# Decoder layer: first projection by column halves of the modulation, key compression earlier in the filler, MLP operands of the second token half in two steps

## Chip, cores, metric

One core of a Trainium2 chip (trn2) runs the whole kernel as one program. The metric is device time in microseconds: the median over runs of the program.

## What is computed

One layer of a decoder trunk, 1024 tokens of width 1024, in float32. Cut to what matters:

```python
mod = silu(c) @ ada_w + ada_b                        # 1024 -> 6 x 1024
sh_a, sc_a, gt_a, sh_m, sc_m, gt_m = split(mod, 6)
h = rmsnorm(x, norm_mix_g) * (1 + sc_a) + sh_a
(a_q, a_k, a_v, b_q, b_k, b_v, b_f, c_q, c_k, c_v,   # 2960 columns in all
 d_q, d_kc, d_vc, d_ks, d_vs, d_kw, d_vw, d_g) = split(h @ w_in)
o_a = diff_attention(rmsnorm(a_q), rmsnorm(a_k), a_v)   # four groups of 4 heads x 64
o_b = forgetting_attention(...)
o_c = stick_breaking_attention(c_q, c_k, c_v)
o_d = native_sparse_attention(...)  # keys compressed: 32 positions, stride 16, @ phi_w
x = x + gt_a * (concat(o_a, o_b, o_c, o_d) @ w_out)
h = rmsnorm(x, norm_ffn_g) * (1 + sc_m) + sh_m
gate, val = split(h @ w_up)                          # 2 x 2816
x = x + gt_m * ((silu(conv3(gate) + conv_b) * val) @ w_down)
```

## The kernel before

**How the order is made.** `Program` records every engine operation in the order in which the code calls it; that number is its priority, to which `K.bias` is added. A list scheduler then fixes an order of instructions for each engine, from planned durations, before the kernel is built; on the chip each engine goes through its list in order. All compute instructions are issued from one recording line, L393 (L400 in the changed file). A tile belongs to a class with a quota (table in lines 547 to 563), and the tiles of one class are handed out in the order in which the program asks for them: in `try_alloc` a tile gets its buffer only if `c["ptr"] == t.order`. Dependencies are found per tile by the byte ranges that operations read and write (`region`). The eight PSUM banks form one group; in the first phase `Xa` and `X` have them, then `S` (4 banks), `T` (2), `O` (1) and `pP` (1), in the end phases `op`, `ox`, `oy`, `up` and `dn`.

**Precision.** An operand of a projection or of the MLP is kept as two tiles, a rounded one (hi) and the remainder (lo), and each product is three matmuls: hi·hi, lo·hi, hi·lo. With eight 128-row pieces of width 1024 (k 0 to 7) a block of 128 tokens takes 24 matmuls per projection.

**Front (lines 637 to 742, 1320 to 1330).** `load_x` brings four blocks of x and normalizes them. `ada_part(1)` loads the 1024 scale columns of `ada_w` in eight tiles `ada` of 128x1024 and sums them, each times a column of silu(c), into `acc` on VectorE; `ada_cols` turns the sum into columns by matmuls with a vector of ones into bank `Xa`. Then `ada_part(0)` does the same for the shift, in the single `acc`. `norm_x` transposes x by `ident` into bank `X`, and `modulate` (736) makes hx on ScalarE and hT hi and lo, the latter on VectorE or GpSimd. The first projections are A's queries (`p_aq`, 256 columns, weights `wh`), A's values (`p_va`, 256, weights `vw`), then 400 columns of C's and D's values with B's forget logits and D's gate logits (`vcd`), then A's keys: each block's sum in an `S` bank. `split_w` (759) makes weights hi on ScalarE and lo on GpSimd. `ada_rest` (1376) mixes the other four parts of the modulation into these projections, one step for 9.0 us of them.

**Attention and its filler.** After that `merge` (1287) mixes the attention of group A, then C, D and B, with `side()` (1393): the remaining projections one after another, `cq`, `ck`, `dk` (D's compressed keys and values and their window parts), `dq`, `cmp` (the compression itself), `vb`, `bq`, `bk`, then the output projection. The sums of these projections go to the one bank `pP`, and so does `pk`, the sum of the compression (line 1067); their raw tiles are of class `nt`. The compression forms X = keys + position embedding on VectorE and multiplies it by `phi` (128 paired matmuls).

**MLP (lines 1465 to 1606).** For each half of the tokens (512), four blocks of the output projection, residual and norm (`xn`), transposes into `oy`, modulation, and `split_b` into operands: `gA` from the first half, and from the second half sums and differences, `gB`, for a scheme of seven products in place of eight. `up_first` makes weights 1 and 2 of an f block (they multiply `gA`), `up_rest` the other five; f 0 and 1 come ahead of the loop (`EARLY`).

## Time and profile before

| | |
|---|---|
| median of 3 runs | 1467.6 us (1467.43 to 1468.78) |
| the profiled execution: its time | 1466.37 us |
| its span | 1464.5 us |
| mean granted TensorE clock | 0.973 |
| PE (matmul) busy | 1375.4 us, 94% of the span |
| PEld (weight load), DVE (VectorE) | 1169.1 us, 1100.9 us |
| ACT (ScalarE), POOL (GpSimd) | 717.6 us, 198.0 us |

PE is TensorE. A busy time is the union of an engine's instructions; idle time is put down to the instruction or transfer whose signal ended it. A share over the whole span is a mean over stages with different limits, so the stages are read one by one: the front to 200 us (modulation, first projections), A and C with the filler, D and B, the turn to the MLP near 811 us, and the MLP to the end. The granted clock is a fraction of TensorE's full 2.4 GHz; it is either full or half of that at a time, and a number between is a mix.

### The profile page before, as it was taken

Reading aid. Unit: us, or ns where it says so; the run is one execution under the profiler, and the core shown is the slowest. Engines: PE = TensorE matmul, PEld = TensorE weight load, DVE = VectorE, ACT = ScalarE, POOL = GpSimd, SP = SyncE. Lnnn points to the kernel's source line nnn. Section 1 sums busy time; section 2 is a strip of 40 time slices with the busy share of each in tenths; the row PEclk is TensorE's granted clock in tenths of the full one; section 3 lists DMA queues with packets and bytes.
Section 4 is the critical chain, followed back from the end, with each engine's and each line's share of the span. In section 5 each row is a group of like instructions: output and inputs, shape, how many; then the busy total and the mean of one; then the engine's idle time right before and its main releaser. Section 6 shows DMA issues by size and latency. Waiting matters only on the chain.

```text
span 1464.5 us, 24046 instructions
## 1 busy us (share of the span) xinstructions
PE 1375.4 (94%) x8573; PEld 1169.1 (80%) x8573; DVE 1100.9 (75%) x2301; ACT 717.6 (49%) x1547; POOL 198.0 (14%) x225
## 2 busy tenths in 40 slices
PE   3999999989799999999999699999999999999998
PEld 2879998888589887787788578888888888888887
DVE  7955669988788987577866976666666665898787
ACT  2530256657587765445754644444334344443242
POOL 4633120222223364100000000000000000000000
PEclk6799999999899999999999899999999999999999
DMA  9579463635421445433335132222222225963665
GB/s 358 198 228 304 153 167 107 179 88 145 122 67 52 123 154 160 143 100 92 82 105 190 64 104 87 77 76 78 86 87 87 83 90 202 373 208 100 230 248 171
DMA packets 169961, 211.22 MB, mean 144 GB/s; under 512 B 25517, under 2 KB 112214, under 8 KB 169842
## 3 DMA queue, kind: packets, MB, share of 16 engines
q1 hardware_dynamic: 168338, 208.52, 45.0%
q0 software_dynamic: 1504, 1.17, 0.4%
q8 instruction: 67, 1.10, 0.3%
q14 instruction: 52, 0.43, 0.1%
HBM read 165.30 MB, written 47.89 MB: 146 GB/s over the span
## 4 chain that ended last, share of the span: by engine, by line
PE 61%; DVE 9%; ACT 2%; issue 1%; DMA 1%; POOL 0%; SPq 0%; POOLq 0%; DVEq 0%; ACTq 0%
PE up L393 29%; PE dn L393 13%; PE T L393 5%; PE pP L393 5%; DVE P L393 4%; PE O L393 3%; PE op L393 3%; PE S L393 3%; ACT P L393 1%; DVE m L393 1%; DVE S L393 1%; DVE pt L393 0%; DVE gB L393 0%; DMA dg<-d_g 0%; PE oy L393 0%
## 5 line engine op out<-in xcount | busy, mean ns | idle before, releaser
L393 PE MATMUL up<-gB,fw 128*128 128x512 f32 x1320 | 306.0, 391 | 12.0 <-DVE fw L393 10.3
L393 PEld LDWEIGHTS up<-gB,fw 128*128 128x128 f32 x1320 | 248.7, 189 | 65.5 <-DVE fw L393 10.8
L393 PE MATMUL dn<-ds 128*128 128x512 f32 x924 | 210.3, 389 | 0.5 <-ACT ds L393 0.3
L393 PEld LDWEIGHTS dn<-ds 128*128 128x128 f32 x924 | 173.1, 188 | 37.4 <-DVE ds L393 1.0
L393 PE MATMUL pP<-wh,hT 128*128 128x256 f32 x1344 | 195.9, 289 | 1.3 <-ACT nt L393 0.7
L393 PEld LDWEIGHTS pP<-wh,hT 128*128 128x128 f32 x1344 | 176.0, 191 | 6.8 <-issue 1.9
L393 ACT ACTIVATE P<-S,nm 128x512 f32<-128x512 f32 (+3 forms) x240 | 135.3, 571 | 76.4 <-DVE nm L393 58.5
L393 PE MATMUL S<-kst,qst 128*128 128x512 f32 (+2 forms) x480 | 135.3, 370 | 6.4 <-DVE P L393 3.2
L393 PE MATMUL T<-ident,P 128*128 128x128 f32 x696 | 112.8, 281 | 17.5 <-ACT P L393 11.3
L393 PE MATMUL up<-gA,fw 128*128 128x512 f32 x528 | 124.5, 390 | 0.0
L393 PEld LDWEIGHTS up<-gA,fw 128*128 128x128 f32 x528 | 98.8, 188 | 20.3
L393 PEld LDWEIGHTS T<-ident,P 128*128 128x128 f32 x696 | 80.3, 141 | 37.0 <-ACT P L393 17.2
L393 PEld LDWEIGHTS S<-kst,qst 128*128 128x128 f32 x480 | 78.6, 193 | 17.3 <-DVE P L393 4.9
L393 ACT COPY pt<-T 128x512 f32<-128x512 f32 (+1 forms) x107 | 57.3, 542 | 61.1 <-PE T L393 59.0
L393 DVE TENSOR_REDUCE m<-S 128x1 f32<-128x512 f32 (+3 forms) x160 | 76.8, 490 | 8.9 <-PE S L393 8.5
L393 ACT CAST ds<-dg 128x512 fp32r<-128x512 f32 x82 | 48.1, 619 | 64.3 <-DVE dg L393 42.4
L393 DVE TENSOR_TENSOR fw<-fr,fw 128x512 fp32r<-128x512 f32 x110 | 75.0, 684 | 0.0
L393 DVE COPY pt<-T 128x512 f32<-128x512 f32 (+1 forms) x93 | 57.0, 623 | 21.4 <-PE T L393 19.9
L393 ACT CAST fw<-fr 128x512 fp32r<-128x512 f32 x110 | 67.5, 614 | 9.0 <-DVE fw L393 8.5
L393 ACT ACTIVATE P<-P 128x128 f32<-128x128 f32 (+8 forms) x98 | 64.8, 690 | 13.7 <-POOL P L393 11.2
L393 ACT COPY u<-up 128x512 f32<-128x512 f32 x44 | 25.9, 588 | 87.5 <-PE up L393 87.5
L393 DVE SCALAR_TENSOR_TENSOR cv<-ga,ccol,cv 128x1023 f32<-128x1023 f32 (+1 forms) x44 | 56.5, 1283 | 15.8 <-ACT cv L393 15.0
(286 smaller groups left out, 2341.1 us busy)
## 6 DMA issues: line engine op xcount, KB each, us to landing
dg<-d_g SPq DMA_DIRECT2D x99, 256.0 KB
fr<-in_ffn_w_up_dram SPq DMA_DIRECT2D x88, 256.0 KB
ada<-in_ada_w_dram SPq DMA_DIRECT2D x64, 256.0 KB
dg<-in_ffn_w_down_dram SPq DMA_DIRECT2D x55, 256.0 KB
d_g<-va SPq DMA_DIRECT2D x22, 512.0 KB
ada<-in_ada_w_dram SPq DMA_DIRECT2D x16, 512.0 KB
wr<-in_w_in_dram SPq DMA_DIRECT2D x32, 256.0 KB
x<-in_x_dram SPq DMA_DIRECT2D x8, 512.0 KB
```

Source lines behind the costliest of these rows:

```text
L393: return getattr(getattr(self.nc, eng), meth)(*a, **k)
```

## The change

1. **Front.** `ada_pair(h)` replaces `ada_part` here: one tile holds shift and scale columns of one half of the 1024 columns (128x2x512), so that eight loads of 512 KB and eight steps on VectorE give what k 0 to 3 of hT need (`pair_cols`), and eight more what k 4 to 7 need. `norm_x` comes in two parts accordingly. `acc` has two buffers.
2. **First projection.** A's queries and keys are one projection of 512 columns (`p_first`, weights in class `vw`), each block's sum in one bank; its weights are made in two steps (`cut`), lo on VectorE. Then come A's values with D's values and the logits (`vd`, 400 columns) and C's values (`CC_V`, 256). hT lo is always on VectorE. `ada_rest` gives one step for 6.0 us.
3. **Filler.** The order becomes `dk`, `cq`, `cmp`, `ck`, `dq`, `vb`, `bq`, `bk`; `pk` is in an `S` bank.
4. **MLP operands.** The second half of the tokens is done as two quarters of 256 columns, `split_b` writing a column range; `up_first(0)` and `up_first(1)` get a priority 300 places earlier. Dependencies know column ranges (`lane`).

The diff, cut to its core:

```diff
@@ class Program: dependencies also by columns
-        return self.p[0], self.p[1], lo, hi
+        return self.p[0], self.p[1], lo, hi, *self.lane
+
+    def columns(self, a, b):
+        v = self[(slice(None),) * len(self.shadow.shape) + (slice(a, b),)]
+        v.lane = a, b
+        return v
@@ classes
-            ("ada", 16, "b", 0), ("acc", 1, "b", 0), ("x", 8, "b", 0), ("hT", 16, "b", 1),
-            ("V", 4, "b", 1), ("VD", 1, "b", 1), ("vw", 8, "b", 1), ("vr", 2, "b", 1),
+            ("ada", 16, "b", 0), ("acc", 2, "b", 0), ("x", 8, "b", 0), ("hT", 16, "b", 1),
+            ("V", 4, "b", 1), ("VD", 1, "b", 1), ("vw", 8, "b", 1), ("vr", 4, "b", 1),
-            ("Xa", 2, "q", 0), ("X", 6, "q", 0), ("S", 4, "q", 1), ("T", 2, "q", 1), ("O", 1, "q", 1), ("pP", 1, "q", 1),
+            ("Xa", 1, "q", 0), ("X", 3, "q", 0), ("S", 4, "q", 1), ("T", 2, "q", 1), ("O", 1, "q", 1), ("pP", 1, "q", 1),
@@ front
+    def ada_pair(h):
+        acc = K.tile("acc", (128, 2, 512))
+        for k in range(8):
+            w = K.tile("ada", (128, 2, 512))
+            K.dma(w, dap(ada_w, k * 128 * 6 * D + h * 512, [[6 * D, 128], [D, 2], [1, 512]]), 524288)
+            if k == 0:
+                K.ts(acc, w, cact[:, k:k + 1], None, OP.mult)
+            else:
+                K.stt(acc, w, cact[:, k:k + 1], acc, OP.mult, OP.add)
+        return acc
+    def pair_cols(h, acc):
+        ps, k = ps1("Xa"), slice(4 * h, 4 * h + 4)
+        for u in (1, 0):
+            for c in range(4):
+                K.mm(ps[:, u * 4 + c:u * 4 + c + 1], acc[:, u, c * 128:(c + 1) * 128], ones[:, 0:1], True, True)
+        K.tt(a1_a[:, k], ps[:, 4:8], b_sc[:, k], OP.add)
+        K.tt(a1_a[:, k], a1_a[:, k], g_sc[:, k], OP.mult)
+        K.tt(sh_a[:, k], ps[:, 0:4], b_ada[:, k], OP.add)
-    def norm_x(half, xns):
-        for k in range(8):
+    def norm_x(half, xns, ks=range(8)):
+        for k in ks:
@@ modulate, split_w, proj
-        K.tt(lo(k, tk), hf, hi(k, tk), OP.subtract, ("DVE", "POOL"))
+        K.tt(lo(k, tk), hf, hi(k, tk), OP.subtract)
-        K.tt(lo, raw, hi, OP.subtract, ("POOL",))
+        K.tt(lo, raw, hi, OP.subtract, (eng,))
-            h, l = split_w(wcls, raw, (128, kp, n))
+            h, l = split_w(wcls, raw, (128, kp, n), "DVE" if cut else "POOL")
+            if cut and k0 + kp == 4:
+                yield 0
@@ first projections
-    p_aq = qk_proj("aq", CA_Q, g_aq, 32, True)
-    p_va = proj([(CA_V, 256)], 256, post_va, "vw", "vr", 4, True)
-    next(p_aq)
-    norm_x(0, x0)
-    next(p_va)
-    steps(p_aq, 4)
+    vd = [(CA_V, 256), (CD_VS, 64), (CD_VW, 64), (CB_F, 4), (CD_G, 12)]
+    p_first = proj([(CA_Q, 512)], 512, post_first, "vw", "vr", 2, True, True)
+    next(p_first)
+    norm_x(0, x0, range(0, 4))
+    acc1 = ada_pair(1)
+    next(p_first)
+    pair_cols(1, acc1)
+    norm_x(0, x0, range(4, 8))
+    steps(p_first, 4)
     norm_x(1, load_x(1))
-    steps(p_va, 4)
-                yield 9.0
+                yield 6.0
-    merge(ahead(p_aq, p_va, proj(vcd, 400, post_vcd, "vw", "vr", 2, True), qk_proj("ak", CA_K, g_ak, 32, True), begun=2),
+    merge(ahead(p_first, proj(vd, 400, post_vd, "vw", "vr", 2, True),
+                proj([(CC_V, 256)], 256, post_vc, early=True), begun=1),
           rest, 1.0)
@@ filler
-        pk = ps1("pP")
+        pk = ps1("S")
-        gs = [("cq", qk_proj("cq", CC_Q, 0.125)), ("ck", qk_proj("ck", CC_K, 1.0)), ("dk", compress()),
-              ("dq", qk_proj("dq", CD_Q, g_dq, 64)), ("cmp", compress_kv()), ("vb", proj([(CB_V, 256)], 256, post_vb)),
+        gs = [("dk", compress()), ("cq", qk_proj("cq", CC_Q, 0.125)), ("cmp", compress_kv()), ("ck", qk_proj("ck", CC_K, 1.0)),
+              ("dq", qk_proj("dq", CD_Q, g_dq, 64)), ("vb", proj([(CB_V, 256)], 256, post_vb)),
@@ MLP operands
-    for half in range(2):
-        xns = []
-        for q in range(4):
+    for half, g0, g1 in ((0, 0, 4), (1, 0, 2), (1, 2, 4)):
+        xns, cw = [], slice(g0 * 128, g1 * 128)
+        for q in range(g0, g1):
-            ps = ps1("oy")
+            ps = ps1("oy")[:, :cw.stop - cw.start]
-                opnd[5][r] = split_b("gB", t1)
+                split_b("gB", t1, 5, r, cw)
     for f in range(EARLY):
+        K.bias = -300.0
         up_first(f)
+        K.bias = 0.0
```

How this moves instructions, at three places.

The front, PE, from its first `Xa` matmuls on; `Xa<-ones,acc` turns a modulation sum into columns, `X<-ident,x` transposes x, `S<-wh,hT` and `S<-vw,hT` are projection products. Before:

```order
L393 MATMUL Xa<-ones,acc 128x1 x8
L393 MATMUL Xa<-ident,hx 128x7
L393 MATMUL Xa<-ones,acc 128x1 x8
L393 MATMUL X<-ident,x 128x128 x8
L393 MATMUL S<-wh,hT 128x256 x96
L393 MATMUL X<-ident,x 128x128 x6
L393 MATMUL S<-vw,hT 128x256 x5
L393 MATMUL X<-ident,x 128x128 x6
```

With the change:

```order
L400 MATMUL Xa<-ones,acc 128x1 x8
L400 MATMUL X<-ident,x 128x128 x16
L400 MATMUL S<-vw,hT 128x512 x39
L400 MATMUL Xa<-ones,acc 128x1 x8
L400 MATMUL S<-vw,hT 128x512 x3
L400 MATMUL Xa<-ident,hx 128x7
L400 MATMUL S<-vw,hT 128x512 x4
L400 MATMUL X<-ident,x 128x128 x4
L400 MATMUL S<-vw,hT 128x512 x50
```

Before, both `Xa` groups (scale, shift) stand ahead of the first product; now 39 products of 512 columns stand between the first and the second group.

The same place on DVE, from the first modulation sum on. With the change:

```order
L400 SCALAR_TENSOR_TENSOR acc<-ada,cact,acc 128x1024 x5
L400 TENSOR_TENSOR vw<-vr,vw 128x1024 x2
L400 TENSOR_TENSOR a_a<-Xa,b_sc 128x4
L400 TENSOR_TENSOR sh_a<-Xa,cols 128x4
L400 TENSOR_SCALAR acc<-ada,cact 128x1024
L400 TENSOR_TENSOR a_a<-a_a,g_sc 128x4
L400 SCALAR_TENSOR_TENSOR acc<-ada,cact,acc 128x1024
L400 CAST hT<-hx 128x512 x2
L400 TENSOR_TENSOR hT<-hx,hT 128x512 x2
```

Before, this place has sixteen sums of 128x1024 ahead of the first hT, and no `vw`; now eight sums of 128x1024, then two halves of the weights' lo, and hT follows two sums into the second pair.

PE around the key compression (`S<-nt,wr` or `pP<-nt,wr`; `V`, `P`, `pt`, `kst`, `qst` are tiles of the attention; `T<-ident,nt 128x32` is the transpose of the position embedding). Before, where it stands among the attention's work, behind all products of `dq`:

```order
L393 MATMUL O<-pt,V 64x128 x6
L393 MATMUL T<-ident,nt 128x128 x4
L393 MATMUL T<-ident,P 128x128 x2
L393 MATMUL S<-kst,qst 128x128 x2
L393 MATMUL T<-ident,P 128x128 x6
L393 MATMUL T<-ident,nt 128x32
L393 MATMUL S<-kst,qst 128x512 x2
L393 MATMUL O<-pt,V 64x128 x8
L393 MATMUL pP<-nt,wr 64x63
L393 MATMUL pP<-wr,nt 63x64
```

With the change, where products of the filler stand just ahead of it and it lies in A's attention:

```order
L400 MATMUL pP<-wh,hT 128x256 x24
L400 MATMUL T<-ident,P 128x128 x3
L400 MATMUL pP<-wh,hT 128x256 x9
L400 MATMUL O<-pt,V 64x128 x4
L400 MATMUL pP<-wh,hT 128x256
L400 MATMUL T<-ident,P 128x128 x6
L400 MATMUL T<-ident,nt 128x32
L400 MATMUL S<-kst,qst 128x512 x3
L400 MATMUL O<-pt,V 64x128 x6
L400 MATMUL S<-nt,wr 64x63
L400 MATMUL S<-wr,nt 63x64
```

The compression went from row 385 of PE's list to row 237, and from bank `pP` to an `S` bank.

PE at the start of the MLP (`op` the output projection, `ox` and `oy` transposes, `up<-gA` products that need the first half of the tokens, `up<-gB` those that need the second). Before:

```order
L393 MATMUL up<-gA,fw 128x512 x6
L393 MATMUL oy<-ident,xn 128x128 x3
L393 MATMUL up<-gA,fw 128x512 x19
L393 MATMUL oy<-ident,xn 128x128 x7
L393 MATMUL up<-gA,fw 128x512 x2
L393 MATMUL oy<-ident,xn 128x128 x4
L393 MATMUL up<-gA,fw 128x512
L393 MATMUL oy<-ident,xn 128x128 x4
L393 MATMUL up<-gA,fw 128x512 x17
L393 MATMUL oy<-ident,xn 128x128 x4
L393 MATMUL up<-gA,fw 128x512 x3
L393 MATMUL up<-gB,fw 128x512 x2
```

With the change:

```order
L400 MATMUL up<-gA,fw 128x512 x12
L400 MATMUL op<-wo,oT 128x512 x22
L400 MATMUL up<-gA,fw 128x512 x24
L400 MATMUL oy<-ident,xn 128x128 x3
L400 MATMUL up<-gA,fw 128x512 x12
L400 MATMUL oy<-ident,xn 128x128 x9
L400 MATMUL up<-gB,fw 128x512
L400 MATMUL oy<-ident,xn 128x128 x2
L400 MATMUL up<-gB,fw 128x512 x2
L400 MATMUL oy<-ident,xn 128x128 x2
L400 MATMUL up<-gB,fw 128x512 x20
```

Before, all products that need `gA` alone stand behind the last product of the output projection; now twelve of them stand ahead of its last 22, and the last transposes are of one quarter of the tokens, 256 columns.

## Rows read from the trace of the kernel before

**Rows 1.** The page, busy time of each engine (its share of the span) and instructions.

```profile
PE 1375.4 (94%) x8573; PEld 1169.1 (80%) x8573; DVE 1100.9 (75%) x2301; ACT 717.6 (49%) x1547; POOL 198.0 (14%) x225
```

**Rows 2.** Windows by stage: busy us of each engine (instructions), granted clock, DMA share, GB/s.

```profile
0.00:50.00 50.00, 22.45 (x100) 20.18 (x101) 39.54 (x70) 22.17 (x44) 25.58 (x34) 0.64 0.98 363
50.00:200.00 150.00, 142.29 (x977) 132.06 (x977) 96.08 (x188) 46.80 (x102) 45.26 (x43) 0.96 0.65 198
200.00:364.00 164.00, 153.13 (x1281) 137.20 (x1281) 146.66 (x481) 106.49 (x318) 31.35 (x34) 0.99 0.49 137
364.00:392.00 28.00, 16.85 (x150) 12.05 (x148) 25.46 (x39) 18.54 (x37) 11.43 (x17) 0.76 0.37 101
392.00:811.00 419.00, 404.64 (x3272) 343.53 (x3272) 313.48 (x793) 249.56 (x603) 84.33 (x99) 1.00 0.40 118
811.00:844.00 33.00, 20.97 (x94) 16.16 (x94) 30.47 (x54) 22.96 (x41) 0.00 (x0) 0.79 0.13 44
844.00:1464.00 620.00, 615.10 (x2710) 507.85 (x2708) 449.22 (x680) 251.10 (x406) 0.00 (x0) 1.00 0.43 140
```

**Rows 3.** Waits of PE: us in total, times, the longest.

```profile
PE Xa L393 <- DVE acc L393: 14.8, 2, 8.4
```

**Rows 4.** Timeline of the front: start us, us, engine, line, what, idle before it.

```profile
15.32 7.96 DVE L393 SCALAR_TENSOR_TENSOR acc<-ada,cact,acc 128x1024 f32<-128x1024 f32 x6
...
40.54 3.33 PE L393 MATMUL S<-wh,hT 128*128 128x256 f32 x14
...
45.98 12.62 PE L393 MATMUL S<-wh,hT 128*128 128x256 f32 x82 [2.11 <-POOL hT L393]
...
75.88 0.68 DVE L393 TENSOR_TENSOR hT<-hx,hT 128x512 fp32r<-128x512 f32 x1
```

**Rows 5.** Lines by form, PE from 0 to 91 us: count, busy us, mean ns, idle before.

```profile
L393 PE MATMUL S<-wh,hT 128*128 128x256 f32 x166 | 26.3, 330 | 2.1 <-POOL hT L393 2.1
...
L393 PE MATMUL S<-vw,hT 128*128 128x256 f32 x96 | 13.5, 290 | 0.0
```

**Rows 6.** The same from 91 to 200 us.

```profile
L393 PE MATMUL S<-vw,hT 128*128 128x400 f32 x192 | 38.5, 363 | 0.0
...
L393 PE MATMUL S<-wh,hT 128*128 128x256 f32 x220 | 28.3, 285 | 0.0
...
L393 PE MATMUL pP<-wh,hT 128*128 128x256 f32 x118 | 14.8, 284 | 0.0
```

**Rows 7.** The same from 844 us to the end, the up-projection.

```profile
L393 PE MATMUL up<-gB,fw 128*128 128x512 f32 x1306 | 299.8, 389 | 0.7 <-ACT u L393 0.7
```

**Rows 8.** Timeline of PE at the third projection.

```profile
112.71 14.86 PE L393 MATMUL S<-vw,hT 128*128 128x400 f32 x80
...
130.04 1.64 PE L393 MATMUL T<-ones,acc 128*128 128x1 f32 x8 [2.47 <-DVE fg L393]
...
131.55 11.15 PE L393 MATMUL S<-vw,hT 128*128 128x400 f32 x46
```

**Rows 9.** Timeline of PE around the key compression.

```profile
361.51 1.56 PE L393 MATMUL pP<-wh,hT 128*128 128x256 f32 x11
...
382.41 0.31 PE L393 MATMUL T<-ident,nt 32*128 32x32 f32 x1
...
385.71 0.36 PE L393 MATMUL pP<-nt,wr 64*64 64x63 f32 x1
```

**Rows 10.** Timeline of PE and DVE at the MLP's start.

```profile
838.09 1.65 PE L393 MATMUL up<-gB,fw 128*128 128x512 f32 x3 [10.33 <-DVE fw L393]
...
843.62 16.63 PE L393 MATMUL up<-gB,fw 128*128 128x512 f32 x71 [0.68 <-ACT u L393]
...
816.10 0.75 DVE L393 TENSOR_SCALAR xn<-x,rms_y 128x1024 f32<-128x1024 f32 x1
...
841.57 0.69 DVE L393 TENSOR_TENSOR gB<-hk,gB 128x512 fp32r<-128x512 f32 x1
```

**Rows 11.** Timeline of DVE: two in a row of 256 columns, and of 512.

```profile
69.22 0.75 DVE L393 TENSOR_TENSOR nt<-nt,qk_y 128x256 f32<-128x256 f32 x2
...
831.94 1.28 DVE L393 TENSOR_TENSOR hf<-hf 128x512 f32<-128x512 f32 x2
```

More of the change, by code (lines that the diff above doesn't have):

```diff
@@ L74, in __init__ @@
         self.t, self.steps = t, steps
+        self.lane = (0, 1 << 30)
         if shadow is None:
@@ L723, in layer_kernel @@
     K.dma(rows[6:7], nsa_knorm_g[0, 1:3].rearrange("(o r) p -> o (r p)", o=1), 512, "POOL")
-    sc_a, = ada_cols(1, [acc], "sc_a", "Xa")
-    a1_a = mod_gain(sc_a, g_mix, "a1_a")
-    vt = ps1("Xa")
-    K.tr(vt[:, :7], rows[0:7], ident[:7, :7])
-    gcols = const([128, 7], name="gcols")
-    K.copy(gcols, vt[:, :7], ("DVE",))
-    for a, f in ((1, -math.sqrt(32.0)), (3, -8.0), (5, -8.0), (6, -8.0)):
-        K.ts(gcols[:, a:a + 1], gcols[:, a:a + 1], f, None, OP.mult)
-    g_aq, g_ak, g_bq, g_bk, g_dq, g_kc, g_sw = (gcols[:, a:a + 1] for a in range(7))
-    acc = ada_part(0)
-    *_, sh_a = ada_cols(0, [acc[:, halves(n)] for n in range(2)], "sh_a", "Xa")
+    pair_cols(0, acc0)
     def modulate(src, k, half, a1, sh, hi, lo, hcls):
@@ L804, in f, with one, rest @@
             K.copy(q, ps.split(256))
+            rest(jj, q)
+        def one(j, ps):
+            if j % 2 == 0:
+                pend.append(K.tile("nt", (128, 2, 256)))
+            K.copy(pend[-1][:, j % 2, :], ps)
+            if j % 2:
+                rest(j // 2, pend[-1])
+        pend = []
+        f.one = one
+        def rest(jj, q):
             if norm:
@@ L967, in layer_kernel @@
     VA = Vals()
-    def post_va(j, ps):
-        K.copy(VA.two(j), ps.split(64))
     def stacks_A(p):
@@ L1318, in steps, with post_first @@
             next(g)
-    vcd = [(CC_V, 256), (CD_VS, 64), (CD_VW, 64), (CB_F, 4), (CD_G, 12)]
-    p_aq = qk_proj("aq", CA_Q, g_aq, 32, True)
-    p_va = proj([(CA_V, 256)], 256, post_va, "vw", "vr", 4, True)
-    next(p_aq)
-    norm_x(0, x0)
-    K.hold = K.ops[-1]
-    next(p_va)
-    K.hold = None
-    steps(p_aq, 4)
+    gcols = const([128, 7], name="gcols")
+    g_aq, g_ak, g_bq, g_bk, g_dq, g_kc, g_sw = (gcols[:, a:a + 1] for a in range(7))
+    post_aq, post_ak = (qk_post([split_out((name, p), s) for p in range(2)], (32, 0)).one
+                        for name, s in (("aq", g_aq), ("ak", g_ak)))
+    def post_first(j, ps):
+        post_aq(j, ps[:, 0:256])
+        post_ak(j, ps[:, 256:512])
+    vd = [(CA_V, 256), (CD_VS, 64), (CD_VW, 64), (CB_F, 4), (CD_G, 12)]
[5 more added lines that the diff above has]
+    pair_cols(1, acc1)
+    vt = ps1("Xa")
+    K.tr(vt[:, :7], rows[0:7], ident[:7, :7])
+    K.copy(gcols, vt[:, :7], ("DVE",))
+    for a, f in ((1, -math.sqrt(32.0)), (3, -8.0), (5, -8.0), (6, -8.0)):
+        K.ts(gcols[:, a:a + 1], gcols[:, a:a + 1], f, None, OP.mult)
+    norm_x(0, x0, range(4, 8))
+    steps(p_first, 4)
     norm_x(1, load_x(1))
@@ L1460, in layer_kernel, with split_b @@
     run_all(fill)
-    def split_b(cls, v):
-        t = K.tile(cls, (128, 2, 512), F32R)
-        K.copy(t[:, 0], v, ("DVE", "ACT"))
-        K.tt(t[:, 1], v, t[:, 0], OP.subtract)
-        return t[:, 0], t[:, 1]
-    kept, opnd = {}, {n: [None] * 4 for n in range(1, 8)}
-    for half in range(2):
-        xns = []
-        for q in range(4):
+    opnd = {n: [None] * 4 for n in range(1, 8)}
+    def split_b(cls, v, n, r, c):
+        if opnd[n][r] is None:
+            t = K.tile(cls, (128, 2, 512), F32R)
+            opnd[n][r] = t[:, 0], t[:, 1]
+        hi, lo = (t[:, c] for t in opnd[n][r])
+        K.copy(hi, v, ("DVE", "ACT"))
+        K.tt(lo, v, hi, OP.subtract)
+    kept = {}
+    for half, g0, g1 in ((0, 0, 4), (1, 0, 2), (1, 2, 4)):
+        xns, cw = [], slice(g0 * 128, g1 * 128)
+        for q in range(g0, g1):
             i = half * 4 + q
```

54 lines of the change are left out of this document (30 added, 24 removed).

## Prediction

> **What bounds the kernel now.** I read the page's first part, then the windows by stage, then the waits of PE, and only then the timelines of the stages where PE is not full. PE is busy 1375.4 of 1464.5 us [rows 1], so some 89 us are all that better order can give. The windows [rows 2] show where they lie: PE works 22.45 of the first 50 us; 16.85 of 28 us between 364 and 392 and 20.97 of 33 us between 811 and 844, in both at a mixed clock (0.76 and 0.79). In the four long stages it is busy for 93 to 99% of the time at a clock of 0.96 to 1.00. The change touches just the three poor stages. The waits put 14.8 us of PE's idle time on the modulation sums of DVE, in two waits [rows 3].
>
> The profiled execution took 1466.37 us, 1.2 us less than the median of 1467.6. I make the sum against it and add 1.2 at the end. About 0.2% (2.9 us) is what a measurement of this kernel can tell from no change.
>
> **Part 1, the front.** Before, eight sums for the scale and eight for the shift run on DVE at 7.96/6 = 1.33 us each, in step with the loads that feed them; the first product starts at 40.54, and after a wait of 2.11 us the steady run begins at 45.98 [rows 4]. The change needs eight loads in place of sixteen before k 0 to 3 can go. Eight tiles end where the scale's eight do now: from the row at 15.32, six sums and what follows end at about 24 us. Behind them DVE does two new instructions, the weights' lo of 1024 columns, by the nearest row 1.33 us each, before the two column steps that hT waits for: about 28 us, and with two transposes' worth of ScalarE and DVE the first product at about 30, against 40.5. That is 10 us of earlier start, but only for half of k: the first four blocks have 48 products of it, 11 us at 0.2296 each [rows 7] and more while the clock is low, say 13; then PE needs the second pair. Its eight loads, also 512 KB each, end where the shift's do now, near 40, plus the sums: hT for k 4 to 7 comes between 48 and 52. The second token half ends on DVE: its last lo is ready at 75.88 + 0.68 before [rows 4]; six of sixteen subtractions on GpSimd return to DVE, and I put it at 78.
>
> So I count what is left at 91 us, where both kernels should be past these waits. Before, 166 + 96 = 262 products of 256 columns are done by 91 us [rows 5], of 576; left are 314 of 256 and 192 of 400 columns. The rows of the next stretch give 28.3/220 = 0.1286 and 38.5/192 = 0.2005 us each [rows 6]: 40.4 + 38.5 = 78.9 us. After, I expect all 192 products of 512 columns done by 91: A's first half by 60, the second by 88 to 91. Left are 192 of 256 and 192 of 400: 24.7 + 38.5 = 63.2 us. The difference is 15.7 us.
>
> It contains a gain that needs no earlier start: 384 products of 256 become 192 of 512. A product of 512 costs 299.8/1306 = 0.2296 us in the MLP [rows 7], so each pair saves 2 x 0.1286 - 0.2296 = 0.0276 us, and 192 pairs save 5.3 us. The filler's products of 256 at 14.8/118 = 0.1254 [rows 6] give 4.1. The Trainium skill speaks against this part: its page "VectorE: DVE Perf Modes", section "The TRN2 errata — SBUF-src ops pay a fixed extra latency per instruction", puts a matmul at 6 cycles plus one per column, so that two of 256 cost 218 ns and one of 512 costs 216; by it the merging would bring 0.5 us and the sum would end 4.8 us higher. The rows disagree with that rule and decide here.
>
> Not all of 15.7 will last. The queues are moved too. SP now issues the weights of the 512 columns (2.1 MB in place of two sets of half) together with the modulation loads, in a stretch where the DMA share is already 0.98 [rows 2]; the bytes up to the first half are the same, only their order is not. DVE gets the weights' lo and six hT, about 2.7 + 4 us of work; it is busy 39.54 of the first 50 us, much of it the sums. The remaining modulation parts come once in 6.0 us of products in place of 9.0, so their matmuls stand earlier in PE's list. The bounds: 3 us (the merging at 4.1 less a microsecond of lag, with the rest lost to DVE) and 18 (what is left plus the 2.11 us wait). I take 13, nearer the count.
>
> What of it reaches the end? In the stretch after, A's attention stands behind the first projections and 118 products of filler (14.8 us [rows 6]); those may shift behind, but PE is full there and its list holds the same work, so a lead of 13 us moves everything after it.
>
> **Part 2, key compression.** The hole at 364 to 392 is a chain: the last product of `dq` into bank `pP` starts at 361.51 and ends 1.56 later; the transpose of the position embedding comes at 382.41, and the first compression product, which has `pP`, at 385.71 [rows 9]. No other filler has a bank between, since `pP` is the only one. In the window PE is idle for 28 - 16.85 = 11.15 us, and of its busy time some 16.85 x 0.24 = 4.0 us is due to the clock of 0.76: 15.2 us in all [rows 2]. DVE is busy 25.46 of 28 us there: the attention's own steps, with the compression's X and copies queued among them. Now `cmp` comes third, in A's stretch, its sum in an `S` bank, so filler products may run in `pP` while the compression waits for X. PE's list has 34 filler products just ahead of it. Its DVE work moves to a stretch where DVE is busy for 146.66 of 164 us [rows 2], 89%, and so has room, not much. The cost of an `S` bank lent: four banks serve the scores; held for 128 paired products, one bank less makes scores wait. The bounds: 0 (the wait only moves) and 15.2 (the hole goes whole). I take 13, as the chain's first member, the bank, is gone, and keep 3 for the scores.
>
> **Part 3, the MLP's start.** PE waits 10.33 us for `gB`, and its steady run begins at 843.62; the last block's xn is made at 816.10 + 0.75, and the last gB is done at 841.57 + 0.69 [rows 10]. The run between is some 36 operations of DVE, 25 us, for all 512 columns (0.60 from start to start; two of 512 take 1.28 [rows 11]). With quarters, half of it is done before the last block's xn, and what remains is as many operations of 256 columns: two take 0.75 [rows 11], 0.34 from start to start, so 36 x 0.34 = 12.2 us in place of some 25. Against that, twelve `up` products stand ahead of the last 22 of the output projection: 12 x 0.2296 = 2.8 us later xn, near 819.6. With the transposes and ScalarE's step ahead of them (842.26 - 816.85 - 36 x 0.60 = 3.8 us now), the last gB would come at about 836 to 837.5, 5 to 6 us earlier, and of the products that could run sooner PE would have done 2 to 3 us more. Gain 8, taken as 7; bounds -3 (the twelve products delay, and the smaller operations win nothing) and 12 (the whole wait with some of the low clock). The column ranges in the dependencies cost nothing on the chip, and `K.bias` for two f blocks only moves weight splits, hidden by idle POOL and ACT.
>
> **Sum.** 1466.4 - 13 - 13 - 7 = 1433.4 us, and 1.2 for the median: about 1435.
>
> **Rivals.**
> - *The front is bound by DVE.* If hT for the second token half is the limit, PE's earlier start is idle again, and only 3 of 13 us stay: 1445. For it: weights' lo and all hT lo are now on DVE; against it: DVE's last lo at 76 us leaves 15 us until 91.
> - *The compression's wait moves into A.* The `S` banks are handed out in program order, so a score that is recorded behind `pk` waits for it, and the `nt` tiles of `ck` and `dq` queue behind those of the compression. Then the chain of 22.6 us (from 363.07 to 385.71 [rows 9]) lies in A's stretch, with none of the gain: 1448. For it: DVE at 89% there; against it: filler and scores both have work ahead of it in PE's list.
> - *MLP quarters bring nothing.* Each DVE step has a fixed part: two of 256 cost 0.68 against 0.60 for one of 512, 36 x 0.08 = 2.9 us, and the twelve products 2.8: 1442. The Trainium skill, same page and section, has the rule behind it: a small operation pays the fixed part again, (N + 151)/0.96 ns for a float32 addition, so 157 ns more for two halves, 5.6 us for 36; rows show half of that.
> - *The gate's loads come too late, and the kernel is slower.* PE reaches the later modulation parts about 13 us sooner, and they are placed every 6.0 us instead of 9.0; PE's queue is in order, so a matmul whose sum is not there stops everything behind it. Such a stop is in the rows now: 2.47 us of wait for a sum, and then 46 products of 400 columns take 11.15 us where 80 took 14.86, 8.55 for 46 [rows 8], 2.6 us of low clock: 5.1 us per late sum. All eight sums late would cost 41 us against a gain of 33: 1475. It decides from the point where loads land after PE's arrival, and turns the sign from the seventh late sum on (7 x 5.1 = 36); DMA share 0.65 after 50 us [rows 2] speaks against it.
>
> **Chances.** The forecast 0.52 (1424 to 1446); front bound by DVE 0.18; compression's wait moves 0.14; MLP nothing 0.10; slower 0.06. Two of the partial cases together would give 1452 to 1456. The range that should hold the time 8 times in 10 is 1420 to 1456: below, the three upper bounds (18 + 15.2 + 12) reach 1422; above, two partial failures. Faster by over 0.2%: all cases but the last and a little, 0.93; within: 0.02; slower: 0.05.
>
> **What would show it.** In the changed kernel's profile, part 1 is right if the first product starts near 30 us and all products of 512 columns of the first projection are done by 91; wrong if PE's wait for hT ends after 80. Part 2 is right if no window of 20 us in A's, C's or D's stretch has PE under 85% busy, and the first compression product waits under 3 us; wrong if a hole like that at 364 appears near it. Part 3 is right if the steady `up` run starts within 18 us of the last xn (26.8 before: 843.62 - 816.85) and the wait for `gB` is under 5 us. The prediction falls if A's stretch grows by over 10 us, or if waits of `T` for a sum add up to over 10 us.

## The result, and the profile after

The changed kernel takes 1450.74 us (median of 4 runs, 1448.44 to 1452.91) against 1467.51 us of the kernel before in the same job: 16.8 us less, a ratio of 0.9888 with a 95% interval of 0.9869 to 0.9908. Forecast were 1435 us and 32.6 us of gain. The profiled execution took 1448.83 us; its span is 1447.1 us, 17.4 less than before. One execution of a kernel below (the weights' lo on GpSimd) took 1938.7 us at a mean granted clock of 0.66 and is left out of its median.

The windows of the changed kernel, columns as in [rows 2]; the first three have borders of that table, the fourth lies in the later part of group C's attention, the fifth is the start of the MLP:

```profile
0.00:50.00 50.00, 29.75 (x124) 24.13 (x125) 39.19 (x80) 20.54 (x37) 11.45 (x27) 0.97 0.99 354
200.00:364.00 164.00, 153.43 (x1390) 138.65 (x1386) 141.88 (x439) 103.30 (x300) 36.57 (x41) 0.99 0.46 128
364.00:392.00 28.00, 26.19 (x220) 24.20 (x219) 23.72 (x41) 20.61 (x37) 4.22 (x11) 1.00 0.26 76
460.00:500.00 40.00, 35.08 (x295) 31.71 (x296) 35.08 (x83) 25.26 (x60) 11.28 (x14) 0.96 0.42 117
783.00:829.00 46.00, 37.93 (x163) 27.11 (x161) 42.23 (x113) 32.78 (x83) 0.00 (x0) 0.96 0.27 94
```

PE works 29.75 of the first 50 us in place of 22.45, and 26.19 of the 28 us from 364 to 392 in place of 16.85: both poor stretches that the prediction spoke of are better at their place. The next row was not foreseen: from 460 to 500 PE is busy for 35.08 of 40 us, where it had 37.75 before (below).

The front, PE and DVE in order of time, against [rows 4]:

```profile
31.40 10.61 PE L400 MATMUL S<-vw,hT 128*128 128x512 f32 x39
...
76.88 0.71 DVE L400 TENSOR_TENSOR hT<-hx,hT 128x512 fp32r<-128x512 f32 x1
...
93.29 3.01 PE L400 MATMUL S<-vw,hT 128*128 128x512 f32 x12
```

The first product starts at 31.40 us (40.54 before, some 30 forecast), the last lo of hT comes at 76.88 + 0.71 (78 forecast), and the last product of the first projection at 96.3 us (91 forecast).

The key compression, PE, against [rows 9]:

```profile
274.49 0.24 PE L400 MATMUL T<-ident,nt 32*128 32x32 f32 x1
...
276.36 0.27 PE L400 MATMUL S<-nt,wr 64*64 64x63 f32 x1
```

The transpose of the position embedding and the first product of the compression are 1.9 us apart with no idle time ahead of either. Before, the transpose came 382.41 - 363.07 = 19.3 us after the last product of `dq`, and the first product another 3.3 us later.

The start of the MLP, PE and DVE, against [rows 10], and PE's waits for the operands and in the front, against [rows 3]:

```profile
800.80 5.32 PE L400 MATMUL op<-wo,oT 128*128 128x512 f32 x22 [2.93 <-DVE oT L400]
...
828.95 16.43 PE L400 MATMUL up<-gB,fw 128*128 128x512 f32 x69
...
813.64 0.74 DVE L400 TENSOR_SCALAR xn<-x,rms_y 128x1024 f32<-128x1024 f32 x1
```

```profile
PE Xa L400 <- DVE acc L400: 6.9, 1, 6.9
...
PE T L400 <- DVE acc L400: 2.5, 3, 1.1
...
PE up L400 <- ACT gB L400: 2.5, 4, 1.4
...
PE up L400 <- DVE gB L400: 0.5, 1, 0.5
```

The steady `up` run starts 828.95 - 814.38 = 14.6 us after the last xn (26.8 before), and the waits for gB are 3.0 us. Before, PE waited 10.33 us at this place, but the row in [rows 10] names `fw` and not `gB` as what ended the wait: the lo of a weight, which VectorE made between its steps for gB, just ahead of PE's start at 838.09:

```profile
837.35 0.68 DVE L393 TENSOR_TENSOR fw<-fs,fw 128x512 fp32r<-128x512 f32 x1
```

So it was a wait for VectorE's list, with gB and weights in it.

### The profile page after: what moved, and what is told of

Its sections match the earlier page's. It is cut to its first block, busy times and chain, and to the rows that moved or that the text cites. A ratio compares the mean times of both kernels' runs of the same rounds, so it can differ in the third digit from the quotient of the medians.

```text
span 1447.1 us, 23711 instructions
## 1 busy us (share of the span) xinstructions
PE 1371.0 (95%) x8381; PEld 1152.1 (80%) x8381; DVE 1100.0 (76%) x2353; ACT 718.0 (50%) x1578; POOL 182.3 (13%) x213
## 4 chain that ended last, share of the span: by engine, by line
PE 51%; DVE 3%; DMA 1%; ACT 0%; issue 0%; SPq 0%; DVEq 0%; ACTq 0%
PE up L400 28%; PE dn L400 14%; PE op L400 3%; PE T L400 2%; PE O L400 2%; PE S L400 1%; DVE gB L400 1%; DVE m L400 0%; DVE hf L400 0%; DMA oin<-o_dram 0%; PE pP L400 0%; PE oy L400 0%; DVE pu L400 0%; ACT P L400 0%; DVE S L400 0%
## 5 line engine op out<-in xcount | busy, mean ns | idle before, releaser
L400 PE MATMUL S<-kst,qst 128*128 128x512 f32 (+2 forms) x480 | 132.3, 367 | 5.8 <-DVE P L400 3.1
L400 PE MATMUL T<-ident,P 128*128 128x128 f32 x696 | 112.0, 279 | 14.6 <-ACT P L400 5.9
L400 PE MATMUL S<-vw,hT 128*128 128x512 f32 (+1 forms) x384 | 91.5, 393 | 0.1
L400 PEld LDWEIGHTS S<-vw,hT 128*128 128x128 f32 x384 | 74.4, 201 | 12.0 <-issue 3.1
L400 ACT COPY pt<-T 128x512 f32<-128x512 f32 (+1 forms) x100 | 53.2, 544 | 59.0 <-PE T L400 56.3
L400 DVE COPY pt<-T 128x512 f32<-128x512 f32 (+1 forms) x100 | 61.1, 622 | 26.4 <-PE T L400 25.9
L400 ACT ACTIVATE P<-P 128x640 f32<-128x640 f32 (+8 forms) x98 | 63.7, 690 | 16.5 <-POOL P L400 13.3
L400 DVE SCALAR_TENSOR_TENSOR acc<-ada,cact,acc 128x512 f32<-128x512 f32 (+1 forms) x70 | 64.2, 918 | 9.8 <-DMA ada<-in_ada_w_dram 8.5
```

Of the source, the lines that this page charges most:

```text
L400: return getattr(getattr(self.nc, eng), meth)(*a, **k)
```

## Experiments

The theories are in the expectations: whether each part wins at its own place and keeps it, who takes it back, and whether the parts have a value of their own at all. A kernel with another program has its order of instructions made anew by the list scheduler, so all of these differ from each other by more than their edit. Gains are against the kernel before in the same job (its medians lie between 1465.8 and 1467.5 us).

| kernel | median us (runs) | before | gain | ratio, 95% interval |
|---|---|---|---|---|
| the change | 1450.74 (4) | 1467.51 | 16.8 | 0.9888, 0.9869 to 0.9908 |
| front alone | 1457.86 (6) | 1465.84 | 8.0 | 0.9950, 0.9934 to 0.9966 |
| compression alone | 1467.82 (12) | 1465.84 | -2.0 | 1.0021, 1.0006 to 1.0036 |
| MLP alone | 1463.50 (12) | 1465.84 | 2.3 | 0.9979, 0.9968 to 0.9990 |
| front and MLP | 1452.30 (6) | 1465.84 | 13.5 | 0.9910, 0.9890 to 0.9929 |
| front and compression | 1452.27 (6) | 1465.83 | 13.6 | 0.9912, 0.9892 to 0.9932 |
| change, `pk` in `pP` | 1457.32 (11) | 1465.83 | 8.5 | 0.9949, 0.9934 to 0.9964 |
| front and MLP, `pk` in `S` | 1462.72 (12) | 1466.56 | 3.8 | 0.9976, 0.9964 to 0.9989 |
| change, VectorE work added in A | 1457.23 (6) | 1466.36 | 9.1 | 0.9941, 0.9921 to 0.9962 |
| change, the same added in B | 1450.29 (6) | 1466.36 | 16.1 | 0.9898, 0.9878 to 0.9918 |
| change, hT lo also on GpSimd | 1454.59 (6) | 1466.36 | 11.8 | 0.9925, 0.9907 to 0.9942 |
| change, weights' lo on GpSimd | 1460.40 (8) | 1466.36 | 6.0 | 0.9960, 0.9939 to 0.9980 |
| change, `pt` on ScalarE | 1448.15 (6) | 1465.83 | 17.7 | 0.9882, 0.9863 to 0.9901 |

### The parts

Front alone: the change with parts 2 and 3 undone, the filler in the order of before and (cut to its core)

```diff
-        pk = ps1("S")
+        pk = ps1("pP")
-    for half, g0, g1 in ((0, 0, 4), (1, 0, 2), (1, 2, 4)):
+    for half in range(2):
-        K.bias = -300.0
```

> Front (part 1) alone on the kernel before. Theory 1 (the parts win at their own place, and part of the front's win is given back in group A's stretch because the compression's VectorE work was moved there): without the moved compression the front keeps what it has at 200 us, about 8 us: 1459.5. Rival 2 (the front's win is small in itself, A's stretch eats it whatever else is there): 4.5 us, 1463. Rival 3 (each new order of the list scheduler moves the time by several us whatever the part): no stable value, a part's gain differs by over 5 us between the kernels with and without the other parts.

It gains 8.0 us, the time that theory 1 gave. Its reason, that the moved compression takes some of this back, falls with the runs below: on the front the compression gains.

Compression alone: the kernel before with only these two of the lines of the diff,

```diff
-        pk = ps1("pP")
+        pk = ps1("S")
-        gs = [("cq", qk_proj("cq", CC_Q, 0.125)), ("ck", qk_proj("ck", CC_K, 1.0)), ("dk", compress()),
-              ("dq", qk_proj("dq", CD_Q, g_dq, 64)), ("cmp", compress_kv()), ("vb", proj([(CB_V, 256)], 256, post_vb)),
+        gs = [("dk", compress()), ("cq", qk_proj("cq", CC_Q, 0.125)), ("cmp", compress_kv()), ("ck", qk_proj("ck", CC_K, 1.0)),
+              ("dq", qk_proj("dq", CD_Q, g_dq, 64)), ("vb", proj([(CB_V, 256)], 256, post_vb)),
```

> Compression and filler order (part 2) alone. Theory 1: with the front as before, A's stretch has nothing to give back, the hole at 364 to 392 goes: 13 us, 1454.5. Rival 2: the hole of 14.6 us goes and 4 to 5 us come back as VectorE-bound waits in C's and D's stretch whatever the front does: 10 us, 1457.5. Rival 3 as before.

Both theories fall: it is 2.0 us slower than before, and not 10 to 13 faster. Yet the hole is closed. These are the windows from 200 to 560 us, first of the kernel before, then of this one (columns as in [rows 2]):

```profile
200.00:300.00 100.00, 94.83 (x799) 84.60 (x799) 91.52 (x324) 65.39 (x198) 15.47 (x13) 1.00 0.54 152
300.00:360.00 60.00, 54.30 (x455) 48.89 (x453) 51.30 (x149) 37.33 (x111) 14.61 (x19) 0.97 0.40 110
360.00:400.00 40.00, 28.85 (x297) 23.20 (x294) 31.42 (x54) 26.45 (x55) 12.71 (x20) 0.83 0.41 119
400.00:460.00 60.00, 57.32 (x494) 51.83 (x493) 51.78 (x81) 44.36 (x87) 15.59 (x34) 1.00 0.25 65
460.00:500.00 40.00, 37.75 (x323) 34.49 (x322) 36.04 (x63) 31.43 (x58) 12.99 (x22) 1.00 0.31 86
500.00:560.00 60.00, 57.92 (x508) 50.83 (x507) 50.90 (x140) 38.52 (x98) 36.00 (x35) 1.00 0.45 137
```

```profile
200.00:300.00 100.00, 90.01 (x797) 78.11 (x796) 90.53 (x301) 60.01 (x179) 17.15 (x15) 0.93 0.46 132
300.00:360.00 60.00, 58.52 (x507) 54.37 (x506) 51.57 (x157) 36.27 (x109) 9.02 (x7) 0.97 0.43 121
360.00:400.00 40.00, 37.94 (x319) 34.75 (x319) 35.38 (x68) 29.82 (x67) 17.57 (x28) 1.00 0.40 119
400.00:460.00 60.00, 55.00 (x466) 48.70 (x465) 51.66 (x85) 47.04 (x95) 16.88 (x36) 1.00 0.33 93
460.00:500.00 40.00, 34.41 (x281) 30.89 (x281) 35.06 (x54) 29.57 (x52) 12.52 (x18) 0.96 0.32 93
500.00:560.00 60.00, 54.18 (x482) 47.13 (x482) 49.15 (x141) 37.39 (x98) 35.50 (x32) 1.00 0.41 125
```

From 360 to 400 PE works 9.1 us more, and from 300 to 360 4.2 more. From 200 to 300 it works 4.8 us less, from 400 to 460 2.3, from 460 to 500 3.3 and from 500 to 560 3.7 less. Over the 360 us PE has 331.0 and 330.1 us, DVE 313.0 and 313.3: the same work in the same time, with PE's idle time in other places. A stretch with borders set by the work says the same: from the last product of the first projections to the first one of the output projection, the kernel before and then this one:

```profile
184.75:559.49 374.74, 345.72 (x2990) 308.70 (x2988) 321.49 (x819) 250.59 (x614) 108.95 (x142) 0.98 0.42 119
```

```profile
182.68:561.17 378.49, 348.54 (x2995) 311.63 (x2993) 325.61 (x828) 250.46 (x617) 111.63 (x140) 0.97 0.41 120
```

PE is idle for 29.0 us of it before and for 30.0 us here. The filler shows it as well; first the kernel before, PE's filler products from 360 to 460 and from 460 to 560 us (count, busy us, mean ns, idle before), and the first product of the output projection by the timeline (start us, us), and SP's loads of the attention's results that it needs, which stand right behind a store of such results:

```profile
L393 PE MATMUL pP<-wh,hT 128*128 128x256 f32 x303 | 43.5, 289 | 0.3 <-ACT V L393 0.3
...
L393 PE MATMUL pP<-wh,hT 128*128 128x256 f32 x298 | 44.6, 289 | 0.0
...
559.49 0.50 PE L393 MATMUL pP<-wo,oT 128*128 128x512 f32 x1
...
544.28 3.48 SPq L393 DMA_DIRECT2D oin<-o_dram  x6
```

And with the compression alone:

```profile
L393 PE MATMUL pP<-wh,hT 128*128 128x256 f32 x403 | 59.8, 288 | 2.3 <-DVE nt L393 1.5 <-DVE V L393 0.8
...
L393 PE MATMUL pP<-wh,hT 128*128 128x256 f32 x240 | 37.5, 298 | 1.3 <-DVE P L393 1.3
...
561.17 0.51 PE L393 MATMUL pP<-wo,oT 128*128 128x512 f32 x1
...
546.49 1.91 SPq L393 DMA_DIRECT2D oin<-o_dram  x4
```

From 360 to 460 it runs 403 products in place of 303, and then has 240 in place of 298 for the next 100 us. They are the last ones: what may follow in bank `pP` is the output projection, which needs group C's attention to be over, and its first product comes at 561.17 us, 1.7 us later than before; the loads ahead of it are 2.2 us later. So group C's attention did not end sooner. What PE did sooner in the hole it lacked at the end of C, where the attention alone has not enough work for it: from 460 to 562 us PE's waits add up to 4.2 us before and to 11.4 here. All this is read from two traces; a run with more filler in stock was not made.

MLP alone (part 3 on the kernel before, with the column ranges of the dependencies; cut to its core):

```diff
-    for half in range(2):
+    for half, g0, g1 in ((0, 0, 4), (1, 0, 2), (1, 2, 4)):
+        K.bias = -300.0
         up_first(f)
+        K.bias = 0.0
```

> MLP operands in two steps and the earlier weights (part 3) alone. Theories 1 and 2 alike: the stretch from the last output products to the steady up run loses 14.7 us in place of 18.3, so 3 to 4 us: 1464. As predicted it would have been 7 us: 1460.5. Rival 3 as before.

2.3 us, a little under the 3 to 4 of theories 1 and 2. Front and MLP without the compression (the filler in the order of before):

```diff
-        pk = ps1("S")
+        pk = ps1("pP")
```

> The change without part 2 (front and MLP only). Theory 1: the front keeps its 8 us, MLP 3.5: 1456. Rival 2: 4.5 and 3.5: 1459.5. Rival 3 as before.

13.5 us, more than any theory gave, and against 16.8 of the whole change: the compression is worth 3.3 us here, with overlapping intervals. The whole without the MLP's part (cut to its core):

```diff
-    for half, g0, g1 in ((0, 0, 4), (1, 0, 2), (1, 2, 4)):
+    for half in range(2):
-        K.bias = -300.0
-        K.bias = 0.0
```

> The change without part 3 (front and compression). With part 3 worth what it is on top of the front alone, 5.6 us (1457.9 to 1452.3): 1456. With what it is on the kernel before, 2.3: 1453. As predicted, 7: 1458.

13.6 us, nearest to the theory that gave 1453. So the compression gives -2.0 us alone, 5.6 on the front, 3.3 on front and MLP; the MLP's part 2.3, 5.5 and 3.2; the front 8.0, and 11.2 and 15.6 on the others. The parts don't add, and rival 3 is right in so far as one and the same edit moves by over 5 us with the order around it. By the intervals it is clear that front and compression gain more together (13.6) than the sum of each alone (6.0); the three values of the MLP's part are not told from each other. Why the compression gains in company isn't settled: in the traces it brings the first product of the output projection from 546.44 to 544.05 us on the front, and from 548.02 to 545.92 on front and MLP, which is 2 us and not the hole's 15.

### Bank and place of the compression

The change with the compression's sum in `pP`, at its new place:

```diff
-        pk = ps1("S")
+        pk = ps1("pP")
```

> The changed kernel with the compression's sum in bank pP again, the order of the filler as changed. If the bank makes the hole (the prediction's chain): a hole of 10 us or more of PE's idle time around the compression, in A's stretch, and the time 5 to 13 us up, 1456 to 1464. If the place alone makes it (theory D: VectorE's queue is what the compression waits for, and filler stands ready elsewhere): within 3 us of the change, 1448 to 1454.

8.5 us of gain in place of 16.8: the bank counts at the new place, and the time is in the range of the first theory. But the hole that it announced does not come. From the last product of the first projections to the first one of the output projection, the change and then this kernel:

```profile
175.32:545.92 370.60, 343.73 (x2991) 307.55 (x2988) 320.86 (x830) 247.57 (x617) 113.08 (x140) 0.99 0.40 113
```

```profile
176.57:556.01 379.44, 351.35 (x2985) 311.71 (x2982) 325.95 (x825) 244.16 (x605) 108.68 (x139) 0.97 0.39 109
```

PE is idle for 26.9 and for 28.1 us. The stretch is 8.8 us longer because PE is busy 7.6 us longer with six products fewer, at a granted clock of 0.97 in place of 0.99. This execution was also 5.0 us above its kernel's median. So the prediction's chain (bank, then wait) is not what these rows show, and what the bank does here stays open. If the bank counts at any place, it does so at the old one: front and MLP of the change, the filler in the old order, and against the kernel of front and MLP only

```diff
-        pk = ps1("pP")
+        pk = ps1("S")
```

> The change without its new filler order: front and MLP as changed, the filler cq, ck, dk, dq, cmp as before, only the compression's sum in an S bank. Base 1452.3 (front and MLP, compression in pP at its old place). Theory B (the place in A costs, the bank gains: with the new order, pP against S measured 6.6 us): products of the next projection run in pP during the compression's wait, 5 to 7 us faster, 1445 to 1447. Theory D (what PE gains in the hole it loses behind, since the attention's chain over VectorE and ScalarE is not shortened): PE's idle time near 364 to 392 shrinks by 8 us or more and the time stays within 2 us, 1450 to 1454.

Both theories miss. It gains 3.8 us, where the same kernel with `pP` gains 13.5: the bank alone costs 9.7 us. Its windows, the last of them also for the same kernel with `pP`, and PE's longest wait here from 420 to 560 us (us in total, times, longest):

```profile
350.00:390.00 40.00, 34.07 (x346) 29.57 (x345) 32.16 (x53) 25.68 (x49) 11.10 (x20) 0.87 0.43 112
390.00:455.00 65.00, 60.04 (x503) 52.94 (x502) 55.63 (x94) 48.46 (x97) 19.44 (x35) 1.00 0.28 70
455.00:500.00 45.00, 34.33 (x269) 30.93 (x268) 38.38 (x58) 26.77 (x49) 16.71 (x19) 0.91 0.35 106
```

```profile
455.00:500.00 45.00, 42.02 (x371) 38.08 (x370) 41.17 (x84) 34.06 (x70) 16.80 (x23) 1.00 0.36 100
```

```profile
PE S L400 <- DVE P L400: 10.2, 5, 4.7
```

The hole is smaller (PE works 34.07 of the 40 us from 350 to 390, and 29.79 with `pP`), and from 455 to 500 PE works 34.33 of 45 us in place of 42.02: it waits 10.2 us for `S` banks that VectorE is still reading. The bank lent to the compression is not the one that is missing, since its last product ends at 375.80 us and its sum is read by 377. It is the same later part of C's attention in which the compression alone had lost its gain; here more is lost than was won. Why this order loses more than it won isn't settled; that the loss is there is what the rows show.

### VectorE's share in it

To see whether VectorE sets the pace of the attention, work of its own was added that nothing needs. In A's attention:

```diff
                     K.stt(P[0], P[1], cf, P[0], OP.mult, OP.add)
+                    K.stt(scr, scr, cf, scr, OP.mult, OP.add)
```

> The changed kernel with 32 added VectorE instructions of 256 columns in group A's attention (none of its results is used), about 0.42 us each, 13.4 us of VectorE. Theory D (from 200 to 560 us VectorE sets the pace, and PE's hole was VectorE's working time, so closing it only moved PE's idle time): most of it comes out at the end, +8 to +13: 1459 to 1464. Rival P (PE and the supply of filler bound this stretch, VectorE has 13% of it free): the added work fits into its gaps, +0 to +4: 1451 to 1455.

And in B's:

```diff
                     exps(P[u], s, rows_min(s, n, cmask), [l[:, c + v:c + v + 1] for v in (0, 8)])
+                    K.stt(scr, scr, l[:, c:c + 1], scr, OP.mult, OP.add)
```

> Control: the same 32 instructions in group B's attention, where PE is over 97% busy and VectorE 60 to 75%. Theory D and rival P alike: hidden, 0 to +3: 1451 to 1454. If it also gives +8 or more, added VectorE work costs its time anywhere, and the run in A tells nothing of A.

The added instructions in the two traces, A's and then B's (count, busy us, mean ns, idle before):

```profile
L400 DVE SCALAR_TENSOR_TENSOR scr<-scr,cf 128x256 f32<-128x256 f32 x32 | 18.6, 580 | 0.0
```

```profile
L400 DVE SCALAR_TENSOR_TENSOR scr<-scr,lb 128x256 f32<-128x256 f32 x32 | 15.3, 478 | 2.3 <-ACT P L400 2.0
```

18.6 us of VectorE in A cost 7.7 us at the end (gain 9.1 in place of 16.8), 15.3 us in B cost nothing that can be told (0.7). So about two fifths of the time added in A came out at the end, between the two theories; 5.9 us of it are there at the first product of the output projection (551.86 us in place of 545.92). Of the time added in B nothing came out; PE is busy 56.04 of the 57 us there (682 to 739 us). The opposite, with work taken from VectorE:

```diff
-                K.copy(pt[:, :w], t[:, :w])
+                K.copy(pt[:, :w], t[:, :w], ("ACT",))
```

> The changed kernel with every copy of transposed probabilities (pt from bank T) on ScalarE; between 178 and 560 us 60 of 107 were on VectorE, 37 us of its 329. The opposite of the run that added VectorE work (13.4 us added, 6.5 came out). Theory D (VectorE sets the pace from 200 to 560): up to half of 37 comes back, 8 to 18 us faster, 1433 to 1443, unless ScalarE, 252 of 382 us busy before and some 280 then, becomes the late one. Rival P (PE and the supply of filler bound it): 0 to 3. Rival A (each copy is waited for, and the free engine of two is the quick one): slower by 3 or more.

One window from 178 to 560 us, of the change and of this kernel:

```profile
178.00:560.00 382.00, 354.12 (x3068) 316.72 (x3066) 328.92 (x854) 251.65 (x628) 114.64 (x139) 0.99 0.40 113
```

```profile
178.00:560.00 382.00, 358.39 (x3097) 320.43 (x3097) 310.29 (x796) 275.06 (x677) 109.08 (x135) 0.98 0.42 116
```

VectorE has 18.6 us less to do, ScalarE 23.4 more, and the gain is 17.7 us in place of 16.8: the fastest kernel of the study, but by the intervals not told apart from the change, as rival P had it. Theory D's 8 to 18 us did not come. Less VectorE work gives little here, more of it costs something. That fits an attention whose length is set by the chain through both engines and not by the throughput of one, but this run does not show it: what VectorE was spared, ScalarE got, and the run does not tell the two apart.

### GpSimd as a helper

hT's lo shared again between VectorE and GpSimd, as before the change:

```diff
-        K.tt(lo(k, tk), hf, hi(k, tk), OP.subtract)
+        K.tt(lo(k, tk), hf, hi(k, tk), OP.subtract, ("DVE", "POOL"))
```

> The changed kernel with hT's lo shared between VectorE and GpSimd again, as before the change. If the second token half of the front is bound by VectorE (18.95 of 20 us from 60 to 80): PE loses 2 to 4 us less in 60 to 100 and the time falls by as much, 1447 to 1449. If GpSimd's longer instruction is the late one: the same or up to 3 us slower.

And the MLP weights of f 0 and 1:

```diff
-        K.tt(l, t, h, OP.subtract)
+        K.tt(l, t, h, OP.subtract, ("POOL",) if f < EARLY else ("DVE",))
```

> The changed kernel with the lo of the MLP weights of f 0 and 1 on GpSimd, idle there, in place of VectorE, 14 instructions of 0.69 us, some 9 us less VectorE work at the MLP's start. If VectorE is what PE waits for there (it is busy 19.5 and 19.9 of 20 us from 800 to 840): 3 to 6 us faster, 1445 to 1448. If the waits are latency of ScalarE and the output projection's order: 0 to 2.

Both are slower than the change, by 5.0 and 10.8 us, which is more than any of the theories gave. The rows of VectorE tell a part of why: first hT's lo in the change and with GpSimd's help, from 26 to 90 us; then a subtraction of `hf` at the MLP's start in the change (780 to 842 us) and with GpSimd at work (787 to 833 us); then one instruction of GpSimd there and one of VectorE beside it, by the timeline:

```profile
L400 DVE TENSOR_TENSOR hT<-hx,hT 128x512 fp32r<-128x512 f32 x16 | 10.8, 687 | 0.1
```

```profile
L400 DVE TENSOR_TENSOR hT<-hx,hT 128x512 fp32r<-128x512 f32 x10 | 9.4, 949 | 0.1
```

```profile
L400 DVE TENSOR_TENSOR hf<-hf 128x256 f32<-128x256 f32 x16 | 6.2, 423 | 0.0
```

```profile
L400 DVE TENSOR_TENSOR hf<-hf 128x256 f32<-128x256 f32 x12 | 7.9, 680 | 0.0
```

```profile
816.19 1.39 POOL L400 TENSOR_TENSOR fw<-fr,fw 128x512 fp32r<-128x512 f32 x1 [2.99 <-ACT fw L400]
...
816.35 1.78 DVE L400 TENSOR_SCALAR xn<-x,rms_y 128x1024 f32<-128x1024 f32 x1
```

Where GpSimd subtracts, VectorE's instructions are longer on the mean: hT's lo 949 ns in place of 687, so that ten of them take 9.4 us where sixteen took 10.8, and `hf` 680 in place of 423. The mean hides two kinds. Of the twelve `hf`, eight take 411 to 424 ns, as in the change; the four that overlap an instruction of GpSimd take 914 to 1507. The `xn` shown takes 1.78 us, the other three there 0.75. So VectorE has hardly less to do. At the MLP's start a wait of 3.1 us of PE for GpSimd's `fw` comes on top. With hT's lo no wait for GpSimd is seen, and the first projections end at 176.28 us in place of 175.32: most of those 5.0 us arise later, where the edit touches nothing.

## Why the prediction was right and wrong

**The range held, and half of the gain was missed.** 1450.7 us lies between 1420 and 1456, the sign was right; the likeliest case's own range, 1424 to 1446, did not hold it. The range was wide enough for one part to fail whole; that it held is no proof of the sum.

**The step that failed: part 2, 13 us for the hole.** The prediction read from the chain at 364 us that the bank `pP` makes the wait, and counted the hole as won. The first half is not borne out: in the change the compression waits for nothing, but with `pP` at the new place no hole comes back either (8.3 us of gain are gone by another way), and `S` at the old place costs 9.7 us. The second half is wrong: alone, this part closes the hole and gives -2.0 us. The filler is a stock that ends at group C's last step, and the attention's chain is not made shorter by giving PE something to do beside it. By the rows of that run the hole was not lost time of the kernel, but time in which PE had nothing that was due: DVE worked 25.46 of those 28 us [rows 2], which the prediction wrote down and did not use. The proper question was when C's attention ends, and whether PE is the bound until then; the first product of the output projection answers it, 559.49 us before and 561.17 with the hole closed. The part's own sign, no window of 20 us with PE under 85% busy, fails too, by little: PE is busy 16.82 of 20 us from 280 to 300 and 16.07 from 460 to 480. The rival "the compression's wait moves into A" was nearest (1448), with its place half right: with the compression alone PE works 4.8 us less from 200 to 300, and the rest went at C's end.

**Part 1: 13 us forecast, 8.0 alone, 11 to 16 with the others.** First product, k 4 to 7 and the last lo came where they were put. In the traces of the kernel before and of the front alone the lead is 13.05 us at the first product of the output projection of A and C (559.49 and 546.44 us), 10.5 at that of B and D (753.64 and 743.15) and 9.3 at the end: the step "a lead of 13 us moves everything after it" does not hold to the end. Two sizes in the front were off. All 192 wide products were to be done by 91 us and were at 96.3, since from 60 to 80 us PE is busy for 16.40 of 20 us and waits most for x (2.4 us), which VectorE makes, itself busy for 18.95; that is the rival of the front bound by DVE, in part. And the merging of q and k was priced at 5.3 us. In the changed kernel's own timeline (start us, us) the products of 512 columns take 9.46/41 = 0.2307 and 6.23/26 = 0.2396 us, those of 256 take 16.58/137 = 0.1210:

```profile
49.73 9.46 PE L400 MATMUL S<-vw,hT 128*128 128x512 f32 x41
...
86.14 6.23 PE L400 MATMUL S<-vw,hT 128*128 128x512 f32 x26
...
150.79 16.58 PE L400 MATMUL S<-wh,hT 128*128 128x256 f32 x137
```

That is 192 x (2 x 0.1210 - 0.2307) = 2.2 us, or 0.5 by the second row. The 0.1286 of [rows 6] came from a stretch whose clock was 0.96 on the mean [rows 2]. An estimate by the Trainium skill's rule for a matmul, which the prediction set aside (page "VectorE: DVE Perf Modes", section "The TRN2 errata — SBUF-src ops pay a fixed extra latency per instruction") is 0.5 us. The trace of the change, with 0.5 and 2.2, lies nearer to it than to 5.3. The clock of 0.64 over the first 50 us [rows 2] was not what kept PE idle there: in the run of the MLP alone, whose front is that of the kernel before, it is 0.97, and PE is busy for 22.68 us in place of 22.45.

**Part 3: 7 us forecast, 2.3 to 5.5 measured.** What was to be seen was seen: 14.6 us from the last xn to the steady run, 3.0 us of waits for gB. But the last xn came later. Counted from the first product of the second half of the output projection (`op`), the last xn ends after 814.38 - 738.28 = 76.1 us in place of 816.85 - 753.64 = 63.2, and the steady run begins after 828.95 - 738.28 = 90.7 in place of 843.62 - 753.64 = 90.0: the run behind xn is shorter because xn itself is 12.9 us later. What was won is that 71 `up` products are done by then in place of 62, nine of 0.23 us, less 0.7: 1.4 us in these two traces. The prediction put this delay at 2.8 us, for the twelve `up` products ahead of the last 22 of the output projection, and found no other price. There was one: the weights pulled ahead by `K.bias` are split on VectorE, which has 42.23 of 46 us to do there; PE waits 2.93 us for oT behind them. "Hidden by idle POOL and ACT" was wrong of the lo, which VectorE makes. It also read PE's 10.33 us as a wait for gB, where the row names a weight's lo, and put 3.8 us ahead of the gB steps down to transposes and ScalarE: VectorE had hardly any idle time there, and five of its 42 operations from 816.77 to 842.26 us were for weights and `ga`. What the quarters give and what the earlier weights give was not run apart.

**The slower rival** (sums of the modulation too late) did not come: PE's waits for `acc` after the front are 2.5 us in all.
